# A two-layer encoder trunk in float32r parts: a quarter of the weights' low parts made by an accumulating DMA

## The chip, the cores and the metric

The kernel runs on one core of one Trainium2 chip. The core has five engines that work side by side: TensorE (PE, matrix products), VectorE (DVE), ScalarE (ACT), GpSimd (POOL) and SyncE (SP, which here only issues transfers). Sixteen DMA engines move data; they serve the queues of SP and of GpSimd alike. The metric is the time of one execution on the device in microseconds (us), the median over the runs. Lower is better.

## What is computed

Two layers of a post-norm encoder on one sequence of 256 tokens with 2048 features. Layer 0 mixes tokens by a stick-breaking attention, layer 1 by a multi-scale pooling.

```python
for i in range(DEPTH):                     # DEPTH = 2, ALPHA = (2 * DEPTH) ** 0.25
    x = layer_norm(ALPHA * x + 0.5 * swiglu(x, *ffn1[i]), *ln1[i])
    x = layer_norm(ALPHA * x + mixers[i](x), *ln2[i])
    x = layer_norm(ALPHA * x + 0.5 * swiglu(x, *ffn2[i]), *ln3[i])

def swiglu(x, w_in, w_out):                # w_in 2048 x 8192, w_out 4096 x 2048
    a, gate = jnp.split(x @ w_in, 2, axis=-1)
    return (jax.nn.silu(a) * gate) @ w_out
```

All is float32. Nearly all of the work is the product of x with about 495 MB of weights, each of which is read once.

## The kernel before, in words

**Parts.** TensorE multiplies in float32r, a float32 with a shortened mantissa. To keep float32's accuracy the kernel writes every operand as the sum of two float32r parts: `hi`, the value rounded, and `lo`, what the rounding left. A product is then hi\*hi + lo\*hi + hi\*lo. For the weights both parts are made on the chip, just ahead of their use.

**Chunks.** `chunk` (L117 of before) takes the next piece of a weight matrix: four tiles of 128 rows by 512 columns, 1 MB, loaded by one DMA on SP's queue into a buffer `raw` (three buffers). It is converted in two halves (j = 0, 1) of two tiles each: ScalarE copies the half to `whi` (a cast that rounds, L133), VectorE subtracts that from the raw half and writes `wlo` (L134). `whi` and `wlo` have five buffers each, so the conversion can run up to four halves ahead of the one in use. A `raw` buffer is free for the next load when both its halves have been converted, a `whi` or `wlo` buffer when TensorE has done its last product with it. There are 468 chunks, 936 halves.

**Products.** `gemm` makes 512 columns of a product, the columns with number `col`: it goes through the chunks r = 0 .. n-1 of the contraction (n = 4 for 2048 features, 8 for 4096) and sums in four PSUM banks, one for each 128 columns (f). In all chunks but the last the order is by tile, then by f, so that a half is used up before the next begins. In the last chunk the order is by f, then by tile, so that the four banks end one after the other and can be evacuated (`evac`); there both halves are in use until the chunk's end. The first products with x ahead of a layer norm sum all three parts in one bank (`one`). The values of the attention (`values`) and the last sublayer (`last`) have loops of their own around `chunk`.

**Around it.** ScalarE and VectorE also evacuate the banks, apply SiLU, the gates and the layer norms, and split x and the inner activations into parts. GpSimd does little: constants at the start, seven small powers for 1 / std (`rstd_of`), and eight transfers that spread the last layer norm's gain and bias over the partitions (`gb`). Each engine runs its instructions in a fixed order; that order is made at build time by a scheduler which plays the program through, from the program's order as the priority, and the waits on semaphores follow from who writes and reads which buffer.

Of the kernel before, what the change touches and what calls it, by code (L numbers as in the profile page):

```python
# [8 lines left out]
F32 = mybir.dt.float32  # L9
F32R = mybir.dt.float32r  # L10
AF = mybir.ActivationFunctionType
ALU = mybir.AluOpType
# [23 lines left out]
def trunk(ctx: ExitStack, tc: tile.TileContext, a: dict, out: bass.AP):  # L36
# [14 lines left out]

# [1 line left out]
    xq = [res.tile([P, 4, T], F32, tag=f"xq{q}", name=f"xq{q}") for q in range(4)]  # L53
    xf = [x[:, j] for x in xq for j in range(4)]
    # Its float32r parts, [hi | lo], each with room for the gain and bias of the layer norm.
    xsq = [res.tile([P, 4, 2, W], F32R, tag=f"xs{q}", name=f"xs{q}") for q in range(4)]
    xs = [x[:, j] for x in xsq for j in range(4)]
    whole = [x[:, :, :T] for x in xs]

# [1 line left out]
    mean_grp = const.tile([P, P], F32, name="mean_grp")  # L61
# [4 lines left out]
    nc.vector.memset(mcol, 1.0 / D)  # L66
    # The tensor engine runs at its full clock only after a while of work: products for
    # nothing, until the first data is here.
    idle = bank("idle")
# [5 lines left out]
    nc.gpsimd.memset(mhalf, -0.5)  # L75
    # tri[k', k] = 1 where k' >= k; past[k, q] = 1 where k < q, twice.
    tri = const.tile([P, P], F32, name="tri")
# [20 lines left out]
    def split(dst, hi_src, lo_src):  # L98
        """dst = [hi | lo] of float32r parts that add up to the source."""
        nc.scalar.copy(dst[:, 0], hi_src)  # L100
        nc.vector.tensor_tensor(out=dst[:, 1], in0=lo_src, in1=dst[:, 0].bitcast(F32), op=ALU.subtract)

    def split2(t, src):
        """xs of tiles t and t + 1, of two tiles side by side."""
        hi, lo = (xsq[t // 4][:, t % 4:t % 4 + 2, h, :T] for h in range(2))
        nc.scalar.copy(hi, src)
        nc.vector.tensor_tensor(out=lo, in0=src, in1=hi.bitcast(F32), op=ALU.subtract)

# [1 line left out]
    def load_x(q, j=None):  # L110
# [4 lines left out]

# [1 line left out]
    def chunk(w, r, c, fine=False, step=4):  # L117
        """Four 128-row tiles of 512 columns of w, in halves of hi and lo parts."""
        raw = raws.tile([P, 4, 512], F32, tag="raw", name="raw")
        if fine:  # L120
            for j in range(4):
                load_x(0, j)
                nc.sync.dma_start(raw[:, j], w[r, c, :, j])
        else:
            for j in range(0, 4, step):
                nc.sync.dma_start(raw[:, j:j + step], w[r, c, :, j:j + step])
        his, los = [], []
        for j in range(2):
            hi = whis.tile([P, 2, 512], F32R, tag="whi", name="whi")
            lo = wlos.tile([P, 2, 512], F32R, tag="wlo", name="wlo")  # L130
            for i in ((slice(0, 1), slice(1, 2)) if step < 4 else (slice(0, 2),)):
                src = raw[:, 2 * j:2 * j + 2][:, i]
                nc.scalar.copy(hi[:, i], src)  # L133
                nc.vector.tensor_tensor(out=lo[:, i], in0=src, in1=hi[:, i].bitcast(F32), op=ALU.subtract)  # L134
            his += [hi[:, i] for i in range(2)]
            los += [lo[:, i] for i in range(2)]
        return his, los

    def gemm(w, col, rhs, evac, hooks=None, load=False, one=0, r0=0):
        """Four 128-row tiles of (a 512-column block of w).T @ x, one bank each: hi*hi + lo*hi left,  # L140
        hi*lo right; or all in one sum of that many columns."""
        nk = len(rhs)
        n = nk // 4
        banks = None

        def mm(ps, hi, lo, f, kk):
            cs = slice(f * P, (f + 1) * P)
            first, last = kk == 0, kk == nk - 1
            x = rhs[kk]
            if one:  # L150
                nc.tensor.matmul(ps[:, :one], hi[:, cs], x[:, 0, :one], start=first, stop=False)  # L151
                nc.tensor.matmul(ps[:, :one], hi[:, cs], x[:, 1, :one], start=False, stop=False)  # L152
                nc.tensor.matmul(ps[:, :one], lo[:, cs], x[:, 0, :one], start=False, stop=last)  # L153
                return

            def high():
                nc.tensor.matmul(ps.rearrange("p (h n) -> p h n", h=2), hi[:, cs], x, start=first, stop=last)  # L157

            def low():
                nc.tensor.matmul(ps[:, :T], lo[:, cs], x[:, 0], start=False, stop=False)  # L160

            for go in ((high, low) if first else (low, high)):
                go()

        for c in range(n):
            if load and c > 0:
                load_x(c)
            his, los = chunk(w, r0 + c, col, fine=load and c == 0, step=2 if load else 4)
            if c == 0:
                banks = [bank(f"ps{f}") for f in range(4)]  # L170
            if c < n - 1:
                for k in range(4):
                    for f in range(4):
                        mm(banks[f], his[k], los[k], f, 4 * c + k)
            else:
                for f in range(4):
                    for k in range(4):
                        mm(banks[f], his[k], los[k], f, 4 * c + k)
                    evac(f, banks[f])
            if hooks and c in hooks:  # L180
                hooks[c]()

    def total(dst, ps, norm=None):
        """dst = left + right half of a product; or, of a raw one, what the layer norm makes of it,
        but for the bias that is returned."""
        if norm is not None:
# [9 lines left out]

# [1 line left out]
    EPS = LN_EPS / (ALPHA * ALPHA)  # L198
# [7 lines left out]
    class Norm:  # L206
        """LN of what x holds, less a shift: its statistics, 1 / std and -mean on all partitions,
        and its result, for four tiles at a time. Ahead of it, xs = [hi | lo] of gain * x."""

# [11 lines left out]
        def add(self, t):  # L221
            """Tiles t and t + 1."""
            q, j = divmod(t, 4)
# [14 lines left out]
        def stats(self):  # L238
            # Sums over the features, by token: means, then mean squares.
            s = self.sums  # L240
# [30 lines left out]
    def sublayer_end(w, rhs, factor, gname, bname, hooks=None, one=0):  # L271
        """x <- LN(ALPHA x + factor y): LN of x + (factor / ALPHA) y, with eps / ALPHA**2."""
        c = factor / ALPHA
# [3 lines left out]
        def shift_down():  # L277
            # The mean of the first group: from here on all is less that shift, which the
            # layer norm doesn't see, and the variance is free of cancellation.
            s0 = tmp.tile([P, T], F32, tag="half", name="s0")  # L280
# [23 lines left out]
    def ahead(norm, products, first=True, last=True):  # L304
        """Products (w, col, evac) with x ahead of its layer norm, which comes meanwhile:
        the statistics in the first of them, the result in the last."""
        for i, (w, col, evac) in enumerate(products):
# [6 lines left out]

# [1 line left out]
    def ffn_in(w_in, norm, hooks=None, npairs=1):  # L316
# [35 lines left out]

# [1 line left out]
    def attention(p, norm):  # L354
# [17 lines left out]
        def diag(x):  # L372
            """The two blocks where only some of the keys are past."""
            return x.rearrange("p (j q) -> p j q", j=3)[:, ::2]

        def scores(hg):
            def go():
                hs = range(4 * hg, 4 * hg + 4)
                with tc.manual_schedule(engines={mybir.EngineType.Activation}):
                    for h in hs:  # L380
                        # By key: keys 0..127 for all queries, keys 128..255 for the later queries.
                        ps = bank(f"z{h}")
# [6 lines left out]
                        nc.scalar.activation(sp[h], zs[h], AF.Abs)  # L389
                    # One table after the other.  # L390
                    for h in hs:
# [3 lines left out]
                for h in hs:  # L395
                    # softplus(z) of the past keys
                    nc.vector.scalar_tensor_tensor(out=sp[h], in0=zs[h], scalar=0.0, in1=sp[h], op0=ALU.max, op1=ALU.add)
# [4 lines left out]
        def weights(hg):  # L402
            def go():
# [7 lines left out]
                for h in hs:  # L411
                    # exp(min(log_w, 0))
                    lw[h] = scratch(28 + h % 4, F32, f"lw{h}")[:, :NZ]
# [38 lines left out]

# [1 line left out]
    def pooling(p, norm):  # L454
# [55 lines left out]

# [1 line left out]
    def last(p, norm):  # L512
# [115 lines left out]
```

## Time and profile before

| | |
|---|---|
| median of 2 runs | 2683.65 us (both runs the same) |
| span of the profiled execution | 2681.8 us; 1.85 us lie around it |
| TensorE products busy | 2666.7 us, 99% |
| TensorE weight loads busy (beside the products) | 2365.1 us, 88% |
| VectorE busy | 1675.7 us, 62% |
| ScalarE busy | 1365.4 us, 51% |
| GpSimd busy | 11.9 us |
| DMA | 499.61 MB, mean 186 GB/s |
| granted TensorE clock | 0.998 of full speed on average |

Busy times are sums over instructions; an engine can be busy without being what the end waits for. A wait names the engine whose work ended it. Times in the views are microseconds from the start of the span; PEld is TensorE's weight load, which runs beside the products.

### The profile page before, as it was taken

Reading aid. Unit: us, or ns where it says so; the run is one execution under the profiler, and the core shown is the slowest. Engines: PE = TensorE matmul, PEld = TensorE weight load, DVE = VectorE, ACT = ScalarE, POOL = GpSimd, SP = SyncE. Lnnn points to the kernel's source line nnn. Section 1 sums busy time; section 2 is a strip of 40 time slices with the busy share of each in tenths; the row PEclk is TensorE's granted clock in tenths of the full one; section 3 lists DMA queues with packets and bytes.
Section 4 is the critical chain, followed back from the end, with each engine's and each line's share of the span. In section 5 each row is a group of like instructions: output and inputs, shape, how many; then the busy total and the mean of one; then the engine's idle time right before and its main releaser. Section 6 shows DMA issues by size and latency. Waiting matters only on the chain.

```text
span 2681.8 us, 38727 instructions
## 1 busy us (share of the span) xinstructions
PE 2666.7 (99%) x15916; PEld 2365.1 (88%) x15916; DVE 1675.7 (62%) x2298; ACT 1365.4 (51%) x1990; POOL 11.9 (0%) x28
## 2 busy tenths in 40 slices
PE   9999999999999999999999999999999999999998
PEld 8888888899999888888988888889888998888886
DVE  6555556585686555565765555667878775555545
ACT  5444444467565444444654444445555565444432
POOL 0000000000000000000000000000000000000000
PEclk9999999999999999999999999999999999999999
DMA  7555555554455555555555555554555545555653
GB/s 255 188 188 187 189 188 189 189 174 162 153 190 183 187 186 186 199 177 201 173 189 189 189 189 189 189 189 170 192 189 176 201 174 182 186 186 187 228 193 126
DMA packets 71521, 499.61 MB, mean 186 GB/s; under 512 B 7984, under 2 KB 8624, under 8 KB 12080
## 3 DMA queue, kind: packets, MB, share of 16 engines
q1 hardware_dynamic: 70704, 495.05, 52.4%
q8 instruction: 124, 2.03, 0.3%
q0 software_dynamic: 640, 2.10, 0.2%
q14 instruction: 53, 0.43, 0.0%
HBM read 495.02 MB, written 2.10 MB: 185 GB/s over the span
## 4 chain that ended last, share of the span: by engine, by line
PE 99%; DVE 1%; DMA 0%; SPq 0%; ACT 0%; issue 0%; DVEq 0%; ACTq 0%
PE ps L157 50%; PE ps L160 26%; PE ps L152 5%; PE ps L151 5%; PE ps L153 5%; PE y L573 2%; PE y L572 2%; PE y L574 2%; PE v L430 1%; PE v L428 1%; PE v L429 1%; DMA xq<-in_x 0%; PE cum L407 0%; DVE z L547 0%; PE bc L257 0%; PE st L244 0%
## 5 line engine op out<-in xcount | busy, mean ns | idle before, releaser
L134 DVE TENSOR_TENSOR wlo<-raw,whi 128x1024 fp32r<-128x1024 f32 (+1 forms) x946 | 1144.3, 1212 | 905.8 <-ACT whi L133 901.2
L133 ACT CAST whi<-raw 128x1024 fp32r<-128x1024 f32 (+1 forms) x946 | 982.0, 1041 | 1080.1 <-PE ps L157 851.9
L157 PE MATMUL ps<-xs,whi 128*128 128x512 f32 x3968 | 1389.8, 396 | 1.1 <-ACT whi L133 0.7
L160 PE MATMUL ps<-xs,wlo 128*128 128x256 f32 x3968 | 1100.5, 280 | 1.0 <-DVE wlo L134 1.0
L157 PEld LDWEIGHTS ps<-xs,whi 128*128 128x128 f32 x3968 | 744.8, 189 | 173.4 <-ACT whi L133 1.0
L160 PEld LDWEIGHTS ps<-xs,wlo 128*128 128x128 f32 x3968 | 748.3, 189 | 7.3 <-DVE wlo L134 1.5
L157 PE MATMUL ps<-g,whi 128*128 128x512 f32 x1536 | 534.9, 394 | 0.0
L160 PE MATMUL ps<-g,wlo 128*128 128x256 f32 x1536 | 427.8, 280 | 0.0
L157 PEld LDWEIGHTS ps<-g,whi 128*128 128x128 f32 x1536 | 287.2, 187 | 65.3
L160 PEld LDWEIGHTS ps<-g,wlo 128*128 128x128 f32 x1536 | 289.7, 189 | 1.1
L152 PE MATMUL ps<-xs,whi 128*128 128x258 f32 (+1 forms) x896 | 252.7, 284 | 0.0
L151 PE MATMUL ps<-xs,whi 128*128 128x258 f32 (+1 forms) x896 | 251.7, 283 | 0.0
L153 PE MATMUL ps<-xs,wlo 128*128 128x258 f32 (+1 forms) x896 | 245.5, 282 | 0.0
L152 PEld LDWEIGHTS ps<-xs,whi 128*128 128x128 f32 x896 | 169.6, 189 | 0.2
L151 PEld LDWEIGHTS ps<-xs,whi 128*128 128x128 f32 x896 | 168.9, 188 | 0.0
L153 PEld LDWEIGHTS ps<-xs,wlo 128*128 128x128 f32 x896 | 167.6, 190 | 0.0
L194 ACT COPY half<-ps 128x256 f32<-128x256 f32 x264 | 97.1, 369 | 121.0 <-PE ps L157 119.6
L572 PE MATMUL y<-wlo,g 128*128 128x512 f32 x256 | 99.6, 389 | 0.0
L573 PE MATMUL y<-whi,g 128*128 128x512 f32 x256 | 99.6, 389 | 0.0
L574 PE MATMUL y<-whi,g 128*128 128x512 f32 x256 | 99.4, 389 | 0.0
L157 PE MATMUL ps<-y,whi 128*128 128x512 f32 x256 | 89.6, 396 | 0.0
L195 DVE TENSOR_TENSOR act<-ps,half 128x256 f32<-128x256 f32 x124 | 52.1, 421 | 46.6 <-ACT half L194 46.6
(151 smaller groups left out, 1677.0 us busy)
## 6 DMA issues: line engine op xcount, KB each, us to landing
raw<-in_l_ffn_w_in SPq DMA_DIRECT2D x252, 1024.0 KB, 4.8
raw<-in_l_ffn_w_out SPq DMA_DIRECT2D x127, 1024.0 KB, 4.8
raw<-in_l_pool_w_in SPq DMA_DIRECT2D x32, 1024.0 KB, 4.9
raw<-in_l_sb_w_qkv SPq DMA_DIRECT2D x24, 1024.0 KB, 4.8
raw<-in_l_pool_w_out SPq DMA_DIRECT2D x16, 1024.0 KB, 4.9
raw<-in_l_sb_w_o SPq DMA_DIRECT2D x8, 1024.0 KB, 4.9
raw<-in_l_pool_w_grp SPq DMA_DIRECT2D x4, 1024.0 KB, 4.9
raw<-in_l_ffn_w_in SPq DMA_DIRECT2D x6, 512.0 KB, 9.4
```

What stands on the lines that cost most here:

```text
L133: nc.scalar.copy(hi[:, i], src)
L134: nc.vector.tensor_tensor(out=lo[:, i], in0=src, in1=hi[:, i].bitcast(F32), op=ALU.subtract)
L151: nc.tensor.matmul(ps[:, :one], hi[:, cs], x[:, 0, :one], start=first, stop=False)
L152: nc.tensor.matmul(ps[:, :one], hi[:, cs], x[:, 1, :one], start=False, stop=False)
L153: nc.tensor.matmul(ps[:, :one], lo[:, cs], x[:, 0, :one], start=False, stop=last)
L157: nc.tensor.matmul(ps.rearrange("p (h n) -> p h n", h=2), hi[:, cs], x, start=first, stop=last)
L160: nc.tensor.matmul(ps[:, :T], lo[:, cs], x[:, 0], start=False, stop=False)
L194: nc.scalar.copy(t, ps[:, T:])
L195: nc.vector.tensor_tensor(out=dst, in0=ps[:, :T], in1=t, op=ALU.add)
L572: nc.tensor.matmul(ps[m], gh, lo, start=kk == 0, stop=False)
L573: nc.tensor.matmul(ps[m], gl, hi, start=False, stop=False)
L574: nc.tensor.matmul(ps[m], gh, hi, start=False, stop=kk == nk - 1)
```

## The change

In the second half of a chunk (j = 1), where r + c is odd (r the chunk's number in the contraction, c the column number) and the chunk is loaded in one piece (step = 4), `lo` is no longer made by VectorE. ScalarE writes the negative of the raw weights to `lo`; since `lo` is float32r, the write rounds, and what lies there is the negative high part. Then a DMA on GpSimd's queue adds the raw weights to it in place (`accum_op=ALU.add`), from the chip's own memory to the same memory: 128 partitions of 1024 elements, 512 KB. 232 of the 936 halves are made so, one in two chunks. The other changed lines only take out comments, so that line numbers behind it differ by five.

```diff
@@ chunk @@
                 src = raw[:, 2 * j:2 * j + 2][:, i]
                 nc.scalar.copy(hi[:, i], src)
-                nc.vector.tensor_tensor(out=lo[:, i], in0=src, in1=hi[:, i].bitcast(F32), op=ALU.subtract)
+                if j == 1 and (r + c) % 2 and step == 4:
+
+                    nc.scalar.activation(lo[:, i], src, AF.Copy, scale=-1.0)
+                    nc.gpsimd.dma_start(lo[:, i], src, accum_op=ALU.add)
+                else:
+                    nc.vector.tensor_tensor(out=lo[:, i], in0=src, in1=hi[:, i].bitcast(F32), op=ALU.subtract)
             his += [hi[:, i] for i in range(2)]
```

The first place is ScalarE in the first feed-forward sublayer, where the even column group 4 is prepared while the group ahead of it ends. `raw` 1765, 1811, 1853, 1895 of before are its four chunks; COPY `half` and CAST `g` belong to the evacuation of the group ahead. Before:

```order
L133 CAST whi_1813<-raw_1811 128x1024
L194 COPY half_1711<-ps0_1571 128x256
L194 COPY half_1727<-ps1_1572 128x256
L100 CAST g12_1709<-gate_1710 128x256
L194 COPY half_1743<-ps2_1573 128x256
L100 CAST g13_1725<-gate_1726 128x256
L133 CAST whi_1817<-raw_1811 128x1024
L194 COPY half_1759<-ps3_1574 128x256
L133 CAST whi_1855<-raw_1853 128x1024
```

And now the same place, where these chunks are `raw` 1779, 1825, 1868, 1910 and the ACTIVATE of L136 writes the negative:

```order
L133 CAST whi_1827<-raw_1825 128x1024
L199 COPY half_1725<-ps0_1584 128x256
L199 COPY half_1741<-ps1_1585 128x256
L100 CAST g12_1723<-gate_1724 128x256
L199 COPY half_1757<-ps2_1586 128x256
L100 CAST g13_1739<-gate_1740 128x256
L136 ACTIVATE wlo_1832<-raw_1825 128x1024
L133 CAST whi_1831<-raw_1825 128x1024
L199 COPY half_1773<-ps3_1587 128x256
L133 CAST whi_1870<-raw_1868 128x1024
```

The negative stands where the cast of that half stood, and the cast comes right behind it.

The second place is ScalarE at the start of the pooling layer, where the layer norm's result is applied (ACTIVATE `xq`, CAST `xs`) while the first products run. Before:

```order
L133 CAST whi_17388<-raw_17386 128x1024
L106 CAST xs0_80<-xq0_76 128x2x256
L218 CAST xs0_80<-vecs_119 128x4x2
L268 ACTIVATE xq2_78<-xq2_78,vecs_119 128x256 x2
L268 ACTIVATE xq3_79<-xq3_79,vecs_119 128x256 x4
L133 CAST whi_17392<-raw_17386 128x1024
L106 CAST xs1_81<-xq1_77 128x2x256
```

And now, with `raw` 17547 for the same chunk:

```order
L133 CAST whi_17549<-raw_17547 128x1024
L106 CAST xs0_80<-xq0_76 128x2x256
L223 CAST xs0_80<-vecs_119 128x4x2
L273 ACTIVATE xq2_78<-xq2_78,vecs_119 128x256 x2
L273 ACTIVATE xq3_79<-xq3_79,vecs_119 128x256 x4
L471 ACTIVATE u_17236<-u_17236,aux_17237 128x256
L133 CAST whi_17553<-raw_17547 128x1024
L106 CAST xs1_81<-xq1_77 128x2x256
L471 ACTIVATE u_17263<-u_17263,aux_17264 128x256
L136 ACTIVATE wlo_17554<-raw_17547 128x1024
```

Here the negative stands behind both casts of its chunk and behind other work; so it does in 41 of the 232 places.

The third place is GpSimd's whole order behind the constants; TENSOR_TENSOR is the power of `rstd_of`, DMA `gb` the gain and bias rows. Before:

```order
L85 AFFINE_SELECT past<-past 128x256
L201 TENSOR_TENSOR rn<-var,mhalf 128x2 x5
L534 DMA gb_23347<-in_l_ln_g 128x512 x4
L534 DMA gb_23352<-in_l_ln_b 128x512 x4
L201 TENSOR_TENSOR rs<-ve,mhalf 128x1 x2
```

And now:

```order
L85 AFFINE_SELECT past<-past 128x256
L137 DMA wlo<-raw 128x1024 x48
L206 TENSOR_TENSOR rn<-var,mhalf 128x2
L137 DMA wlo<-raw 128x1024 x16
L206 TENSOR_TENSOR rn<-var,mhalf 128x2
L137 DMA wlo<-raw 128x1024 x48
```

The transfers of the low parts stand between the powers, in the order of the chunks.

## Rows read from the trace of the kernel before

**Rows 1.** Page, part 1: busy us, share of the span, count, by engine
```profile
PE 2666.7 (99%) x15916; PEld 2365.1 (88%) x15916; DVE 1675.7 (62%) x2298; ACT 1365.4 (51%) x1990; POOL 11.9 (0%) x28
```

**Rows 2.** Page, part 4: the chain that ended last, by engine
```profile
PE 99%; DVE 1%; DMA 0%; SPq 0%; ACT 0%; issue 0%; DVEq 0%; ACTq 0%
```

**Rows 3.** Waits: who waited for whom; us in total, times, longest
```profile
DVE wlo L134 <- ACT whi L133: 901.2, 667, 5.1
ACT whi L133 <- PE ps L157: 851.9, 562, 4.2
...
PE ps L160 <- DVE wlo L134: 1.0, 1, 1.0
```

**Rows 4.** Groups by line and shape: count, busy us, mean ns, idle before
```profile
L134 DVE TENSOR_TENSOR wlo<-raw,whi 128x1024 fp32r<-128x1024 f32 x926 | 1131.2, 1223 | 898.9 <-ACT whi L133 894.6
...
L133 ACT CAST whi<-raw 128x1024 fp32r<-128x1024 f32 x926 | 970.4, 1050 | 1071.9 <-PE ps L157 851.9 <-PE y L574 93.8 <-PE ps L152 91.8
```

**Rows 5.** Page, parts 3 and 6: the load queue's share; one load, us to landing
```profile
q1 hardware_dynamic: 70704, 495.05, 52.4%
...
raw<-in_l_ffn_w_in SPq DMA_DIRECT2D x252, 1024.0 KB, 4.8
```

**Rows 6.** Timeline, ScalarE, even column group: start, us, instruction, idle before
```profile
188.46 1.05 ACT L133 CAST whi<-raw 128x1024 fp32r<-128x1024 f32 x1
...
197.57 1.05 ACT L133 CAST whi<-raw 128x1024 fp32r<-128x1024 f32 x1 [1.76 <-PE ps L157]
200.43 1.05 ACT L133 CAST whi<-raw 128x1024 fp32r<-128x1024 f32 x1 [1.81 <-PE ps L157]
```

**Rows 7.** Timeline, weight loads: first use of those two low parts
```profile
197.14 0.19 PEld L160 LDWEIGHTS ps<-xs,wlo 128*128 128x128 f32 x1
...
206.26 0.19 PEld L160 LDWEIGHTS ps<-xs,wlo 128*128 128x128 f32 x1
```

**Rows 8.** Timeline, ScalarE, odd column group: casts of the halves concerned
```profile
225.65 1.05 ACT L133 CAST whi<-raw 128x1024 fp32r<-128x1024 f32 x1 [1.72 <-PE ps L157]
...
236.89 1.05 ACT L133 CAST whi<-raw 128x1024 fp32r<-128x1024 f32 x1 [0.94 <-PE ps L157]
```

**Rows 9.** Timeline, weight loads: first use of those two low parts
```profile
236.46 0.19 PEld L160 LDWEIGHTS ps<-xs,wlo 128*128 128x128 f32 x1
...
247.68 0.19 PEld L160 LDWEIGHTS ps<-xs,wlo 128*128 128x128 f32 x1
```

**Rows 10.** Timeline, GpSimd: the first four issues of the gain rows
```profile
2479.26 2.35 POOL L534 DMA_DIRECT2D gb<-in_l_ln_g  x4 [334.72 <-PE ps L157]
```

**Rows 11.** DMA queues, 2479.3 to 2482.5: packets, MB, share of 16 engines
```profile
q1 hardware_dynamic: 133, 1.02, 86.2%
```

**Rows 12.** DMA queues, 2482.5 to 2488: the software queue
```profile
q0 software_dynamic: 320, 1.05, 63.9%
```

**Rows 13.** Tile gb: its transfers, from issue to landing
```profile
DMA to landing us min/median/max: 6.2/6.9/8.2
```

**Rows 14.** DMA queues, 180 to 212: the load queue
```profile
q1 hardware_dynamic: 818, 5.92, 51.6%
```

**Rows 15.** Timeline, ScalarE: casts of three halves with short windows
```profile
30.78 2.00 ACT L133 CAST whi<-raw 128x1024 fp32r<-128x1024 f32 x2
...
1918.66 1.06 ACT L133 CAST whi<-raw 128x1024 fp32r<-128x1024 f32 x1 [0.58 <-PE ps L157]
...
2650.93 1.05 ACT L133 CAST whi<-raw 128x1024 fp32r<-128x1024 f32 x1 [1.67 <-PE y L574]
```

**Rows 16.** Timeline, weight loads: first use of those three low parts
```profile
39.92 0.19 PEld L160 LDWEIGHTS ps<-xs,wlo 128*128 128x128 f32 x1
...
1924.21 0.19 PEld L160 LDWEIGHTS ps<-xs,wlo 128*128 128x128 f32 x1
...
2658.67 0.19 PEld L572 LDWEIGHTS y<-wlo,g 128*128 128x128 f32 x1
```

## Prediction

> **What bounds the kernel now.** I read the busy shares first. TensorE works 99% of the span, VectorE and ScalarE about half of it [rows 1]. The chain that ended last says the same in another way: 99% of it is TensorE [rows 2]. So an instruction saved elsewhere is worth nothing unless TensorE waits for it. The waits give the direction: VectorE waits 901 us in all for ScalarE's high parts, ScalarE 852 us for TensorE to give back a buffer, while TensorE waits 1.0 us, once, for a low part [rows 3]. The preparation of weights runs as far ahead as its five buffers allow and then stands still. TensorE's whole idle time is 2681.8 - 2666.7 = 15 us, and no change can win more than that, 0.6%.
>
> What matters for this change is therefore a single number: how long a low part may take before TensorE wants it. I call it the window: from the end of the moment at which the negative can be written to the weight load that first reads that low part. The negative needs the raw weights and a free buffer, just as the cast of the high part does, so it can start when the cast of that half started before. In a gemm with an even column number the transferred halves are those of its second and fourth chunk. The cast of the first of these began at 188.46 and took 1.05 [rows 6], the weight load came at 197.14 [rows 7]: window 7.6 us. For the other one, 197.57 + 1.05 to 206.26: 7.6 again. In a gemm with an odd column number it is the first and third chunk: 225.65 + 1.05 to 236.46 and 236.89 + 1.05 to 247.68 [rows 8, 9], both 9.7 us. The even windows are shorter because the last chunk of a product is used four columns at a time, so that both its halves come free only at its end, and because a fourth chunk's second half is wanted early for the same reason. By the loops, 116 transfers are of even columns and 116 of odd ones.
>
> Some windows are shorter still, where ScalarE is late with the cast: I compared the start of the cast with the first weight load for all 232 halves, and 13 lie below 7.3 us. The first in time is the second cast of the pair that begins at 30.78 (it ends at 32.78, used at 39.92: 7.1), the shortest begins at 1918.66 (used at 1924.21: 4.5), the last at 2650.93 (used at 2658.67: 6.7) [rows 15, 16].
>
> **The change part by part.** VectorE loses 232 subtractions of 1223 ns [rows 4], 284 us; it was idle for more than that, so this is worth 0. ScalarE gets 232 more instructions. The negative has the cast's shape, which takes 1050 ns, so 244 us, 51% to 60% of the span. It stood waiting for TensorE 852 us, which covers this: 0. In the regular groups the order shows the negative ahead of its own half's cast, so the cast comes 1.05 us later, with a window of its own that is over a microsecond longer than the one I worked out for the low part. Where the order has the negative behind both casts and other work (41 of 232 places, mostly at the layer norms), its window shrinks by another 1.05.
>
> GpSimd issues 232 transfers. Four issues of the gain rows took 2.35 us [rows 10], 0.6 each, 140 us in all on an engine that was empty: 0. Its seven small power steps now stand behind such issues; at worst each is held for one half's time, 2.9 us (197.57 to 200.43 [rows 6]), some 20 us; I take 0, since one issue takes 0.6.
>
> The DMA engines carry 0.524 MB (512 KB) more per transfer. In a quiet stretch the hardware queue moved 5.92 MB in 51.6% of 32 us, 359 GB/s [rows 14]: a plain copy would keep all sixteen busy for 1.46 us. An accumulating one isn't in this trace. From below it costs that copy. From above: with n copies' worth per transfer the engines' share becomes 52.4% [rows 5] + n x 232 x 1.46 / 2682 = 52.4% + 12.6% n, full at n = 3.8. I take n = 2, because two streams have to be read (raw and the negative) for one that is written: 2.9 us, share 78%.
>
> The Trainium skill (Collectives: The Full Stack, The bandwidth ceiling: the fold count and why AG ≠ RS ≠ AR) says that an add inside the DMA is free but needs two source reads, and gives 32.35 against 62.28 GB/s for the two. By that estimate n would be 1.9 and a landing 0.1 us shorter than with my 2; no run here shows it.
>
> A transfer from GpSimd's queue also starts late. The first gain row was issued at 2479.26 [rows 10], and up to 2482.5 only the hardware queue has packets [rows 11]; after that the software queue has 1.05 MB [rows 12]. That is 3.2 us from issue to first packet. So landing after the negative: 3.2 + 2.9 + 0.3 for the hand-over and the report of the end (my estimate) = 6.4 us; bounds 3.2 + 1.5 + 0.3 = 5.0 below, 3.2 + 5.5 (n = 3.8) + 0.3 = 9.0 above. The nearest measured thing, a 256 KB row transfer on that queue with loads beside it, landed in 6.2 to 8.2 us [rows 13].
>
> The Trainium skill (DMA: Bandwidth & Descriptors, Anatomy of one DMA) fits such a transfer with 2.0 us plus its bytes at 436 GB/s, 3.2 us for 512 KB. The trace disagrees: 3.2 us pass here before a first packet moves, so the row is used. By the page's estimate hardly a window would be missed.
>
> Collisions: loads are issued in order, and a raw buffer is now free only when its transfer has landed. In an even group the first transfer lands at 189.5 + 6.4 = 195.9; two loads of 2.9 us each then go at once. A load lands in 4.8 us [rows 5], so about 1.9 pass before its packets: they flow from 197.8 to 203.6. The second transfer's packets start at 198.6 + 3.3 = 201.9 and share 1.7 us: 0.9 later, landing at 205.9, needed at 206.26. It fits, narrowly. In odd groups 2 us and more remain. A late load has slack too: landing at 200.7 it meets the cast that started at 200.43 before [rows 6], and that half too is wanted more than eight microseconds later.
>
> The sum: subtraction 0, negative 0, issues 0, regular windows 0. The 13 short windows have their middle at 5.8, about 5.1 with the negative behind the cast: 13 x (6.4 - 5.1) = 17 us. The profiled execution (span 2681.8, 1.85 around it) is the median run itself: 2683.65 + 17 = 2700.
>
> **What a miss costs.** Within a pair the second transfer starts before the first one's stall, so its need moves with the stall and the pair pays once. Every microsecond of landing past 7.6 costs 58 pairs x 1 us = 58 us, past 9.7 twice that. 2% is 54 us, about what a measurement of this kernel can tell from no change; it is reached at a landing of about 8.2 us.
>
> **The rivals.**
> Slower: the transfer takes a quarter of a copy's rate (n = 4). Then it needs 5.8 us, lands 9.3 after the negative, 1.7 late in the even columns: 58 x 1.7 = 99, and 13 x 4.2 = 55 at the short windows, 2840 us. The queues would stand at 103%, which alone means 2760. For it speaks that the margin of my forecast is 1.2 us in one place and 0.4 in another; against it, that nothing in an addition asks for four passes. It decides from a landing of 8.2 us on. Chance 0.23.
> Much slower: landing at 12 us (many small descriptors, or a longer start than that of a plain transfer): 58 x 4.4 + 58 x 2.3 + 13 x 7 = 480, about 3160 us. Nothing in the trace excludes it, as no accumulating transfer is in it. Chance 0.18.
> Faster: VectorE's relief reaches TensorE. At most 15 us of idle time exist, so 2668 at best; over 2% can't come from there. Chance 0.02.
>
> **How the numbers follow.** Forecast (landing 5 to about 8 us; 2680 to 2735) 0.57, slower 0.23, much slower 0.18, faster 0.02. I give 2700. The range reaches from 2680 over the first slower case, to 2860, and leaves out the much slower one. Faster by over 2%: 0.02; within 2%: 0.57; slower: 0.41.
>
> **What the new profile would show.** Right: low-part transfers landing in 6 to 7 us from issue, DMA share between 65 and 80%, TensorE's waits for the transfer under 30 us and at the layer norms and the pooling layer, VectorE near 1390 us busy, ScalarE near 1610. Wrong: waits of TensorE for the low part in every even group (rate or start mis-sized, visible as landing over 7.6), a DMA share near 100% (n of 4 or more), or waits for power steps behind GpSimd's issues.

## The result, and the profile after

| | before | after |
|---|---|---|
| median | 2683.65 us | 2729.25 us (2 runs, 2725.56 and 2732.94) |
| ratio | | 1.017, 95% interval 1.0153 to 1.0187 |
| profiled execution, its span | 2681.8 us | 2723.9 us (time 2725.56) |

The change costs 46 us, 1.7%. That lies under the 2% bound and inside the forecast's own range (2680 to 2735), but it is nearly three times the 16 us of the sum. The page of the changed kernel: part 1 (busy us by engine), part 3 (queues: packets, MB, share of 16 engines), part 4 (the chain that ended last), groups of part 5, and part 6 (issues, KB, us to landing).

```profile
PE 2677.0 (98%) x15916; PEld 2367.0 (87%) x15916; DVE 1407.1 (52%) x2066; ACT 1571.4 (58%) x2222; POOL 212.9 (8%) x260
...
q1 hardware_dynamic: 70704, 495.05, 51.2%
q0 software_dynamic: 34048, 123.75, 23.3%
...
PE 85%; DMA 9%; issue 3%; ACT 2%; DVE 1%; SPq 0%; DVEq 0%; POOLq 0%; ACTq 0%; POOL 0%
...
L137 POOL DMA_DIRECT2D wlo<-raw x232 | 201.1, 867 | 2465.7 <-ACT wlo L136 1620.5
...
L136 ACT ACTIVATE wlo<-raw 128x1024 fp32r<-128x1024 f32 x232 | 245.5, 1058 | 152.0 <-PE ps L165 135.2
...
raw<-in_l_ffn_w_in SPq DMA_DIRECT2D x252, 1024.0 KB, 5.6
...
wlo<-raw POOLq DMA_DIRECT2D x232, 512.0 KB, 5.8
```

The engines are as forecast: VectorE 1407 us (about 1390 was said), ScalarE 1571 (1610), the DMA share 51.2 + 23.3 = 74.5% (78%). What is new is in the chain: 99% TensorE before [rows 2], now 85%, with 9% of DMA. The waits of the changed kernel (who for whom: us in total, times, longest) and the landing times of the tile `wlo` tell which DMA:

```profile
ACT whi L133 <- PE ps L162: 382.8, 275, 6.3
ACT whi L133 <- DMA raw<-in_l_ffn_w_in: 140.2, 54, 4.9
...
PE ps L165 <- DMA wlo<-raw: 20.5, 16, 3.6
...
POOL rn L206 <- DVE var L256: 9.0, 4, 2.3
...
PE ps L158 <- DMA wlo<-raw: 6.2, 4, 2.6
...
PE y L577 <- DMA wlo<-raw: 3.9, 2, 2.5
```

```profile
DMA to landing us min/median/max: 4.5/5.8/11.4
```

TensorE waits 20.5 + 6.2 + 3.9 = 30.6 us for transfers, 22 times, where it waited 1.0 us for a low part before [rows 3]. A landing takes from 4.5 to 11.4 us after its issue. ScalarE, which stood before a full buffer for 852 us [rows 3], now does so for 383, and also waits for loads; TensorE itself waits 1.0 us, once, for a high part.

The last product ends 41.8 us later than before (2711.7 against 2669.9). 30.6 us of that are these waits. Some 5 us are lost where the granted clock fell behind three of them; I have not traced the other 6 singly. The stretches around the first fall, all engines (length; busy us and count of PE, PEld, DVE, ACT and POOL; granted clock, DMA share, GB/s), and products there:

```profile
601.00:603.00 2.00, 2.00 (x18) 1.83 (x16) 2.00 (x6) 1.10 (x5) 0.00 (x0) 1.00 1.02 287
605.70:609.10 3.40, 3.40 (x16) 3.40 (x17) 0.72 (x3) 0.74 (x2) 0.86 (x1) 0.50 1.04 373
609.20:611.20 2.00, 2.00 (x19) 2.00 (x18) 0.94 (x1) 2.00 (x4) 0.00 (x0) 1.00 1.00 225
```

```profile
605.60 1.20 PE L158 MATMUL ps<-xs,wlo 128*128 128x256 f32 x4 [2.56 <-DMA wlo<-raw]
606.59 0.41 PE L156 MATMUL ps<-xs,whi 128*128 128x256 f32 x1
...
609.36 0.28 PE L158 MATMUL ps<-xs,wlo 128*128 128x256 f32 x1
```

TensorE had stood 2.56 us for a transfer; then 0.50 was granted (1.2 of 2.4 GHz) from 605.7 to 609.1, products began every 0.21 us in place of 0.12, and 16 x 0.09, about 1.5 us, were lost on top of the wait. The same happened after the waits of 3.63 us (at 1908.9) and 2.97 us (2086.9). The kernel before has no such fall between its start and its end.

### The profile page after: what moved, and what is told of

Same layout as the page of the kernel before. It is cut to its first block, busy times and chain, and to the rows that moved or that the text cites. A ratio compares the mean times of both kernels' runs of the same rounds, so it can differ in the third digit from the quotient of the medians.

```text
span 2723.9 us, 39725 instructions
## 1 busy us (share of the span) xinstructions
PE 2677.0 (98%) x15916; PEld 2367.0 (87%) x15916; DVE 1407.1 (52%) x2066; ACT 1571.4 (58%) x2222; POOL 212.9 (8%) x260
## 3 DMA queue, kind: packets, MB, share of 16 engines
q1 hardware_dynamic: 70704, 495.05, 51.2%
q0 software_dynamic: 34048, 123.75, 23.3%
## 4 chain that ended last, share of the span: by engine, by line
PE 85%; DMA 9%; issue 3%; ACT 2%; DVE 1%; SPq 0%; DVEq 0%; POOLq 0%; ACTq 0%; POOL 0%
PE ps L162 45%; PE ps L165 23%; DMA wlo<-raw 7%; PE ps L158 3%; PE ps L157 3%; PE ps L156 3%; PE y L577 2%; PE y L578 2%; PE y L579 2%; DMA raw<-in_l_ffn_w_in 1%; DMA raw<-in_l_ffn_w_out 1%; ACT whi L133 1%; ACT wlo L136 1%; PE v L435 1%; PE v L433 1%
## 5 line engine op out<-in xcount | busy, mean ns | idle before, releaser
L139 DVE TENSOR_TENSOR wlo<-raw,whi 128x1024 fp32r<-128x1024 f32 (+1 forms) x714 | 859.6, 1208 | 1094.0 <-ACT whi L133 1088.1
L165 PE MATMUL ps<-xs,wlo 128*128 128x256 f32 x3968 | 1102.1, 281 | 13.4 <-DMA wlo<-raw 11.5
L137 POOL DMA_DIRECT2D wlo<-raw x232 | 201.1, 867 | 2465.7 <-ACT wlo L136 1620.5
L136 ACT ACTIVATE wlo<-raw 128x1024 fp32r<-128x1024 f32 x232 | 245.5, 1058 | 152.0 <-PE ps L165 135.2
```

The costliest lines, as they stand in the source:

```text
L136: nc.scalar.activation(lo[:, i], src, AF.Copy, scale=-1.0)
L137: nc.gpsimd.dma_start(lo[:, i], src, accum_op=ALU.add)
```

## Where the long landings come from

A regular even column group, that of [rows 6, 7]: timelines of ScalarE, GpSimd and the weight loads (start, us, instruction, idle before), then the software queue from 191 to 196, with one transfer in it.

```profile
189.33 1.06 ACT L136 ACTIVATE wlo<-raw 128x1024 fp32r<-128x1024 f32 x1
...
198.29 1.06 ACT L136 ACTIVATE wlo<-raw 128x1024 fp32r<-128x1024 f32 x1 [1.52 <-PE ps L165]
```

```profile
190.69 0.87 POOL L137 DMA_DIRECT2D wlo<-raw  x1 [18.24 <-ACT wlo L136]
199.65 0.87 POOL L137 DMA_DIRECT2D wlo<-raw  x1 [8.09 <-ACT wlo L136]
```

```profile
198.09 0.19 PEld L165 LDWEIGHTS ps<-xs,wlo 128*128 128x128 f32 x1
...
207.22 0.19 PEld L165 LDWEIGHTS ps<-xs,wlo 128*128 128x128 f32 x1
```

```profile
q0 software_dynamic: 144, 0.52, 55.0%
```

The negatives end at 190.39 and 199.35, so the windows are 7.7 and 7.9 us: the forecast's 7.6. The first transfer, alone, lands 4.5 us after its issue. Its packets fill the engines for 55% of 5 us, 2.75 us; start and report take the other 1.75. The second shares the engines with a load and lands 6.2 after its issue, 6.5 after the negative (7.3 was forecast), 1.4 before its use. Both fit, and by such groups the change would cost nothing.

An odd column group fits as well, as long as it begins well: at 227.72 to 261.42 four transfers land within 5.0 to 5.5 us, and windows are 10.0. But another one of the same form, from 983.54 on, looks so (GpSimd's issues, then SP's load issues):

```profile
983.54 0.86 POOL L137 DMA_DIRECT2D wlo<-raw  x1 [4.75 <-ACT wlo L136]
994.78 0.86 POOL L137 DMA_DIRECT2D wlo<-raw  x1 [10.38 <-DVE gate L339]
1006.12 0.86 POOL L137 DMA_DIRECT2D wlo<-raw  x1 [10.48 <-ACT wlo L136]
1018.19 0.86 POOL L137 DMA_DIRECT2D wlo<-raw  x1 [11.21 <-ACT wlo L136]
```

```profile
993.58 0.80 SPq L126 DMA_DIRECT2D raw<-in_l_ffn_w_in  x2
...
1004.75 0.80 SPq L126 DMA_DIRECT2D raw<-in_l_ffn_w_in  x2
...
1016.27 0.81 SPq L126 DMA_DIRECT2D raw<-in_l_ffn_w_in  x2
```

The first transfer starts beside a load (issued at 983.34) and lands 9.9 us after its issue, at 993.4. Until then it holds a raw buffer, and SP's queue, which runs in order, holds the next load too. At 993.58 both loads, 2 MB, go out, 1.2 us ahead of the next transfer, which now shares the engines with them through its whole way and lands after 9.8 us, at 1004.6; at 1004.75 the next pair of loads goes out. The delay reproduces itself from chunk to chunk. Of the 48 landings of over 8.9 us, 40 had a pair of loads issued 0.2 to 3.5 us ahead of the transfer. 35 of the 48 lie in odd columns, most of them in the window of 10 us, where they are just in time: TensorE waits 0.4 us in all for odd columns with such a window. The last chunk of an even column has about 8 us, and there they are not in time. One such place is the last chunk of column 2 in the first feed-forward sublayer's second product. Its transfer goes out 1.5 and 1.1 us behind a pair of loads, lands after 10.05 us and finds a window of 8.3 (GpSimd, TensorE):

```profile
491.51 0.87 POOL L137 DMA_DIRECT2D wlo<-raw  x1 [10.07 <-ACT wlo L136]
```

```profile
501.61 0.38 PE L165 MATMUL ps<-g,wlo 128*128 128x256 f32 x1 [2.07 <-DMA wlo<-raw]
```

TensorE waits 13.1 us in all in ten such chunks, 14.6 in seven places with windows under 7.3 us, and 3.0 in the rest. The longest landing of all is near the end of the kernel (SP, GpSimd, TensorE; then the queues from 2565 to 2577):

```profile
2564.59 0.80 SPq L126 DMA_DIRECT2D raw<-in_l_ffn_w_out  x2
```

```profile
2565.35 0.86 POOL L137 DMA_DIRECT2D wlo<-raw  x1 [9.22 <-ACT wlo L136]
```

```profile
2576.77 0.50 PE L577 MATMUL y<-wlo,g 128*128 128x512 f32 x1 [2.46 <-DMA wlo<-raw]
```

```profile
q1 hardware_dynamic: 288, 2.10, 53.2%
q0 software_dynamic: 262, 1.00, 41.7%
```

Loads and transfers (the next one is issued at 2572.53) have the engines busy for 95% of these 12 us between them, and the transfer of 2565.35 takes 11.4 us where a lone one takes 4.5. The Trainium skill (Trainium Kernel Development and Optimization, Key Constraints) says that transfers of all issuing queues run on the same sixteen engines and interleave; these rows agree.

My theory: the loss is the lengthening of landings by loads beside them, a small part short windows, and on top the falls of the clock behind long waits. Rivals: ScalarE's extra work or the changed order; the transfer by itself; a fixed cost of every transfer. The trace gives the theory its size: with a landing 4.8 us after the negative in every window of the changed kernel, about 6 of the 30.6 us of waits would be left.

## The experiments

Edits are against the changed kernel. Every kernel was timed against the kernel before, on the same chip (before: 2683.5 to 2683.9 us).

**The negative alone.** The transfer is left out, so `lo` stays the negative high part, and the raw weights are never added to it.

```diff
-                    nc.gpsimd.dma_start(lo[:, i], src, accum_op=ALU.add)
```

> The transfer is left out; ScalarE still writes the negative, so that a quarter of the low parts are the negative high parts and the product is not the reference's. It shows what ScalarE's 232 extra instructions and the new order cost by themselves. Theories A and B: within 4 us of the kernel before, 2680 to 2688, and no granted clock under full speed between start and end. Theory C (ScalarE's extra work or its order makes TensorE wait): 2695 or more.

Measured: 2683.23 us, ratio 0.9999 (0.9990 to 1.0009), no wait of TensorE over 1.2 us. So ScalarE's 245 us, the order, and VectorE's relief together are worth nothing, in either direction. All of the loss hangs on the transfers.

**A copy in place of the addition.** `lo` is then the raw weights: same bytes written, same starts.

```diff
-                    nc.gpsimd.dma_start(lo[:, i], src, accum_op=ALU.add)
+                    nc.gpsimd.dma_start(lo[:, i], src)
```

> The transfer copies the raw weights over the negative instead of adding to it, so a quarter of the low parts are wrong; ScalarE's work, issues and waits stay. It measures the price of the addition. If the add costs a second read: packets of the software queue go from 328 ns to about 160, its share of the DMA engines from 23% to about 12%, landing alone from 4.5 to about 3.2 us, and TensorE's waits to under half (below 12 us), 2690 to 2700. If the start of a transfer from GpSimd's queue is what costs: landing stays at 4 us or more and the time within 10 us of the changed kernel, 2715 or more.

Measured: 2692.95 us, ratio 1.0037 (1.0022 to 1.0052). The queue's row of that kernel, and its landings:

```profile
q0 software_dynamic: 34048, 123.75, 12.7%
```

```profile
DMA to landing us min/median/max: 2.9/3.7/8.1
```

```profile
PE ps L165 <- DMA wlo<-raw: 5.4, 2, 4.6
...
PE ps L158 <- DMA wlo<-raw: 1.2, 1, 1.2
```

Without the gain rows (0.2%) the copy keeps all engines busy for 12.5% x 2690.8 / 232 = 1.45 us, just the 1.46 worked out from [rows 14]; the addition for 23.1% x 2723.9 / 232 = 2.71, 1.87 times as long. That is about what a second read would add, though no view shows the reads as such. Waits for transfers fall to 6.6 us, and four fifths of the loss go. The clock falls once, at the wait of 4.6 us.

**The first half in place of the second.** My first idea of the collisions was that the second half's transfer, which holds the raw buffer to the end, brings the pairs of loads about. With the first half the chunk's own second cast comes later, and windows should be 10 us nearly everywhere.

```diff
-                if j == 1 and (r + c) % 2 and step == 4:
+                if j == 0 and (r + c) % 2 and step == 4:
```

> The transfer makes the low part of the first half of the same chunks (j = 0) instead of the second. Each low part is still made in full; nothing else is moved. A raw buffer is then held mainly by VectorE's second half, as before the change, so loads are no longer held back by a transfer and should not go out in pairs. Theory A (TensorE's new waits come mostly from transfers that meet two weight loads on the DMA engines): nearly all landings between 4.5 and 6 us from issue (changed kernel: median 5.8, up to 11.4), TensorE waits for transfers under 8 us in all, time 2685 to 2695. Theory B (the transfer by itself is too long for its windows): landings spread as in the changed kernel, 2700 to 2720. Theory C (ScalarE writes the negative too late at the layer norms): landings near 4.5 to 6, but some 13 us of waits stay at the layer norms and the pooling layer, 2695 to 2705.

Measured: 2717.96 us, ratio 1.0126 (1.0105 to 1.0146). Windows did grow (median 9.97; in even columns 10.0 in place of 7.9), but landings grew with them and TensorE waits 23.6 us for transfers. Its landings:

```profile
DMA to landing us min/median/max: 4.5/6.8/11.3
```

Theory A missed: the time is in theory B's range, the landings spread as B said, and this run alone could not tell the two apart; the one without loads, below, decides. The idea that the hold to the end of the chunk is the one cause of the collisions falls: 200 of the 232 landings now take over 6 us, against 105 in the changed kernel.

**Own low buffers.** Transferred halves get two low buffers of their own, the others the remaining three, so that the negative can be written a chunk earlier.

```diff
-    wlos = ctx.enter_context(tc.tile_pool(name="wlos", bufs=5))
+    wlos = ctx.enter_context(tc.tile_pool(name="wlos", bufs=3))
+    sums_ = ctx.enter_context(tc.tile_pool(name="sums_", bufs=2))
...
-            lo = wlos.tile([P, 2, 512], F32R, tag="wlo", name="wlo")
+            moved = j == 1 and (r + c) % 2 and step == 4
+            lo = (sums_ if moved else wlos).tile([P, 2, 512], F32R, tag="wlo", name="wlo")
```

> The low parts that a transfer makes get two buffers of their own, and three are left for the others (five in all, as in the changed kernel). The negative then needn't wait for the buffer of five halves ago and can be written as soon as the raw weights are there; the loads are held back by the landing as in the changed kernel. Theory A (collisions with loads): landings still spread up to 9 us and more, but the windows are 2 to 5 us longer, so TensorE's waits fall under 10 us, 2685 to 2697. Theory B (transfer by itself too long): the same fall. Theory C (ScalarE late): waits of some 13 us stay at the layer norms, 2697 to 2710.

Measured: 2691.24 us, ratio 1.0033 (1.0020 to 1.0046). Landings are as long as before (4.5/6.1/11.5), but the windows, from the end of the negative to the weight load, have their middle at 13.3 us in place of 9.7. No product waits for a transfer, and a weight load does so once:

```profile
PEld ps L167 <- DMA wlo<-raw: 0.3, 1, 0.3
```

No clock fall is left. The last product ends at 2670.7, against 2669.9 before. What remains is behind it: 17.5 us to the end in place of 11.9. I put that down to the last chunks' lack of low buffers; the next run tries it.

**Own low buffers, shared out anew at the end.** As above (the diff is against that version, whose own pool is called `moved_lo` here), but a late chunk of the last sublayer takes the buffer of its second half from those of the transferred halves.

```diff
-            lo = (sums_ if moved else wlos).tile([P, 2, 512], F32R, tag="wlo", name="wlo")
+            lo = (moved_lo if moved or (spare and j == 1) else wlos).tile([P, 2, 512], F32R, tag="wlo", name="wlo")
...
+                parts = chunk(w_out, cc, q, step=2 if q == 3 and cc == n - 1 else 4, spare=q == 3 and cc == n - 3)
```

> The transferred halves have two low-part buffers of their own, the rest the other three, and in the last four chunks of the last sublayer the halves share them in such a way that five stand ready at the end, as in the kernel before. With its own buffers alone the transfers cost 8 us, 5.6 of it behind the last product (17.5 us in place of 11.9). Theory: wider windows (middle 12 us in place of 8.5) outlast the longest landing of 11.4 us, TensorE waits for no transfer, the tail is 11.9 us again, time 2684 to 2687, ratio to the kernel before 1.000 to 1.001. Rival: the tail comes from the transfers beside the last loads and not from the buffers, then it stays near 17 us and the time at 2690.

Measured: 2690.0 us (2686.95 to 2696.74, 9 runs), ratio 1.0025 (1.0015 to 1.0034). The profiled execution is the fastest one, 2686.95: TensorE waits 0.5 us for transfers and ends 1.3 us later than before, and the tail is 14.1 us, between the two expectations. The median is the rival's 2690, not the theory's 2684 to 2687. What the other executions, up to 10 us slower, lose stays open, and with it how much of the tail came from the buffers. It doesn't beat the kernel before, and by the 15 us of idle time it couldn't by much.

**Without loads.** After the first gemm the same weight tiles stay in SBUF and are read again: all casts, negatives, transfers and products remain.

```diff
-    raws = ctx.enter_context(tc.tile_pool(name="raws", bufs=3))
+    raws = ctx.enter_context(tc.tile_pool(name="raws", bufs=1))
...
+        plain = not fine and step == 4
+        if plain and len(kept) == 2:
+            raw = kept[turn[0] % 2]
+            turn[0] += 1
+        else:
+            raw = (keep if plain else raws).tile([P, 4, 512], F32, tag=f"k{len(kept)}" if plain else "raw", name="raw")
...
+        if plain:
+            pass
...
```

> The changed kernel without its weight loads: every gemm after the first reads two weight tiles that stay in SBUF, so the products are of wrong weights and the output is not the reference's; the casts, negatives, transfers, subtractions and all products are made as before. It tells whether the long landings of the changed kernel come from the loads that run beside the transfers. Theory (collision): all landings at 4.5 to 4.7 us from issue, none over 6; TensorE's waits for a transfer fall from 30.6 us to at most 8 (with a landing of 4.5 in every window of the changed kernel's trace, 6.3 us would be left), the granted clock stays whole, time 2684 to 2695. Rival (the transfers are slow by themselves, or held up by GpSimd's or ScalarE's work): landings spread up to 10 us as before, waits stay near 30 us, time 2715 to 2730.

Measured: 2702.07 us, ratio 1.0068 (1.0052 to 1.0083): slower than the theory said, faster than the rival. The landings have their middle at 4.5 us, three quarters of them under 4.6 and 11 of 232 over 6 (up to 6.7), where the theory had none; the waits for transfers, 6.2 us in four places, are the theory's. The clock did not stay whole: it fell behind the waits of 1.73 us (at 1357.2) and 2.34 us (at 1902.7). But this version had a single raw buffer for its start, and 10.9 of its 20.7 us at the last product were lost before 40 us, with TensorE standing 8.7 us at 22.5 for VectorE. So once more with three:

```diff
...
+        if plain and len(kept) == 3:
+            raw = kept[turn[0] % 3]
+            turn[0] += 1
+        else:
+            raw = raws.tile([P, 4, 512], F32, tag="raw", name="raw")
...
```

> The kernel without weight loads again, with three raw buffers at the start as the changed kernel has (the first version had one, and its trace shows 10.9 us lost before 40 us, while the first products' weights came in one at a time). After the first gemm the three tiles stay and are read in turn; the products are of wrong weights, all instructions but the loads are there. Collision theory: what is left of the loss is the short windows alone, 6 to 9 us: landings 4.5 us, TensorE's waits for transfers 5 to 8 us, one or two falls of the granted clock at 1.7 us each, no loss before 40 us; time 2689 to 2694. Rival (the 10.9 us belong to the transfers and not to the missing buffers): 2699 to 2704 again.

Measured: 2691.19 us (2690.46 to 2693.59, 7 runs), ratio 1.0030 (1.0018 to 1.0041). Landings and waits of that kernel:

```profile
DMA to landing us min/median/max: 4.5/4.5/6.4
```

```profile
PE ps L176 <- DMA wlo<-raw: 5.9, 4, 2.3
...
PE ps L169 <- DMA wlo<-raw: 1.0, 2, 0.8
```

6.9 us of waits, 7.3 us of loss, no fall of the clock (its longest waits for transfers are 1.75 and 2.28 us), and nothing over 0.5 us lost before 40 us, so the rival falls. The windows are those of the changed kernel (middle 9.8 and 9.7 us), so it is the landings that differ: without loads beside them the same transfers cost 7 us, with them 46.

**Half the bytes.** One of the two tiles of a half goes by the transfer, VectorE adds the other to the negative.

```diff
-                    nc.gpsimd.dma_start(lo[:, i], src, accum_op=ALU.add)
+                    nc.gpsimd.dma_start(lo[:, :1], src[:, :1], accum_op=ALU.add)
+                    nc.vector.tensor_tensor(out=lo[:, 1:], in0=src[:, 1:], in1=lo[:, 1:].bitcast(F32), op=ALU.add)
```

> Only the first of the two tiles of a transferred half (256 KB) goes by the accumulating transfer, the other is added by VectorE to the negative that ScalarE wrote. Half the bytes in the same 232 places, with the same starts. Collision theory: a landing alone 3.1 us (4.5 less half of the 2.7 us in which packets flow), beside loads 4 to 7; TensorE's waits for a transfer less than half of 30.6 us, no fall of the granted clock, time 2690 to 2702. Rival (a start or a fixed cost of each transfer sets the stalls): landings shorter by under 1 us, waits over 20 us, time over 2712.

Measured: 2691.68 us, ratio 1.0030 (1.0019 to 1.0041).

```profile
DMA to landing us min/median/max: 3.2/3.8/7.7
```

```profile
PE ps L166 <- DMA wlo<-raw: 3.0, 3, 2.2
...
PE ps L159 <- DMA wlo<-raw: 2.3, 2, 2.0
```

The waits for transfers are 5.3 us, under a fifth of 30.6, though as many transfers start at the same places. A fixed cost of each is not what stalls TensorE. Past the first 12 us the clock fell once all the same, behind the wait of 2.2 us (at 1348.0), where no fall was expected.

**Twice as many.** The second half of every chunk is transferred, 463 in all.

```diff
-                if j == 1 and (r + c) % 2 and step == 4:
+                if j == 1 and step == 4:
```

> The second half of every chunk goes by the transfer, not of every other one: twice as many, about 464, half of all low parts. DMA share by the changed kernel's rows: 51% of loads and two times 23% of transfers, 98%. Collision theory: loads and transfers always lie beside each other, landings mostly 8 to 11 us, beyond the windows of 7.6 and 9.7 us in many groups; TensorE waits in most gemms, the DMA engines become the bound or nearly so, time 2800 to 2950. Rival (a stall belongs to a transfer and not to what lies beside it): the loss just doubles, 46 us to about 92, 2775 us, landings with the same middle of 5.8 us.

Measured: 2958.55 us (2946.41 to 2970.81), ratio 1.1025 (1.0994 to 1.1056). The chain of that kernel, and the largest group of TensorE's waits:

```profile
DMA 47%; PE 33%; issue 13%; ACT 4%; DVE 2%; POOL 0%; SPq 0%; POOLq 0%; ACTq 0%; DVEq 0%
```

```profile
PE ps L165 <- DMA wlo<-raw: 132.4, 101, 5.7
```

Twice the transfers cost six times as much, 275 us, a little more than the theory's range. The middle landing is 6.9 us, not the 8 to 11 that I expected, and the DMA share 92.5%; the clock falls 29 times. Loss by transfer is no constant: it grows with what lies beside it on the engines.

## Why the prediction was off

**What held.** TensorE is the bound, and nothing saved elsewhere is worth anything: the negative alone shows 0 for the subtraction and for ScalarE. So is GpSimd's issue, though it took 0.87 us, not 0.6 from [rows 10]. The power steps do not wait behind issues: they wait for VectorE, as before. The windows were right to 0.3 us, 7.7 to 10.0. The transfer's weight was right: n = 2 was taken, 1.87 measured. The estimate of 1.9 from the Trainium skill (Collectives: The Full Stack, The bandwidth ceiling: the fold count and why AG ≠ RS ≠ AR) agrees with what the copy and the addition show here.

**The start was mis-sized, to the good side.** The 3.2 us before the first packet came from the gain rows [rows 10 to 12]. The transfers of this change needed 1.75 us for start and report together, so that a lone landing is 0.3 + 4.5 = 4.8 us after the negative, not 6.4. (The 0.3 for the hand-over stood there without a row; measured from the end of the negative to the issue it is 0.3.) The prediction set aside the estimate of the Trainium skill (DMA: Bandwidth & Descriptors, Anatomy of one DMA) of 3.2 us for a plain 512 KB; the copy's 2.9 us is near that estimate. Why the gain rows start later wasn't tried.

**The short windows** were charged 17 us. The kernel without loads shows what they cost at a lone landing, 7 us: 13 such windows were counted, only six of them stalled, as the landing was shorter.

**The step that failed is the one on collisions, which put the regular windows at 0 in the sum.** It had the mechanism (a raw buffer held until the landing, two loads going out at once) and worked it through in one even group, where it found 0.9 us (6.2 - 4.5 = 1.7 measured) and the second transfer in time ("it fits, narrowly"). It took that one group for all, and said that in odd groups 2 us and more remain. In the changed kernel nothing remains in many odd groups: the loads are held until just before the next transfer, the collision lasts for the whole transfer, and the long landing sets up the next, 9 to 10 us in a window of 10. They cost TensorE only 0.4 us themselves, but the same chain runs on into even columns and through the longer products, and at their last chunk the narrow fit breaks: landings of 8.1 to 11.4 us in nine of the ten places where TensorE waits there, with 6.4 in the sum. Windows of 7.3 us and more, charged 0, cost 16.1 of the 30.6 us of waits, 13.1 of it in last chunks of even columns; the short ones cost 14.6, of which about 6 would be left at a lone landing. The price is the difference between 46 and 7 us, 38 us. In the profiled execution it stands as 30.6 - 6.9 = 24 us of waits, 3 x 1.5 = 5 us at the lowered clock, and some 5 us not traced singly. That the repetition is due to the hold alone is read from times in the trace; no run isolated it, and the run with the first half shows that collisions come also where the transfer is not the chunk's last.

**What was missing altogether** is that a long wait can cost more than itself by the clock; those 5 us are part of the 38. The two errors to either side (10 us too much for the short windows, 38 too little for collisions) bring 2700 to about 2729. That this still lies inside 2680 to 2735 is in part luck, since the one hides some of the other. None of the rivals came: the rate was not a quarter, and the landing not 12 us in the middle, but its upper tail reached 11.4, and a tail is enough where TensorE is 99% busy. One sum was off, too: by its own terms the forecast reaches 54 us at a landing of 7.9 us, not 8.2 (13 x (7.9 - 5.1) + 58 x (7.9 - 7.6)).

## What to carry to other kernels

Where a DMA is put between two engines' work, compare the window with the landing beside the largest transfers that can run at that moment, not with the mean share of the queues; 75% of the engines were in use here and landings still more than doubled. Ask what buffer the transfer holds, whose load waits for it, and whether that load then starts just ahead of the next transfer: such a delay can feed itself, as at 983 us here. A cure is a longer window (buffers of its own for what is transferred) or smaller transfers, and each took the loss here from 46 to 8 us; neither gave a gain, since the engine that was relieved was not the bound.

## What the runs showed of the hardware

- An accumulating transfer of 512 KB within SBUF took 4.5 us alone, a copying one 2.9 us, an accumulating one of 256 KB 3.2 us. GpSimd issued the accumulating ones in 0.86 to 0.87 us, the copy in 0.53.
- Beside weight loads the accumulating one took up to 11.4 us in the changed kernel, and a load issued 0.3 us ahead of it 11.3.
- Behind some single waits of TensorE the granted clock fell to 0.5 (1.2 of 2.4 GHz): in the changed kernel behind 2.56, 2.97 and 3.63 us, in the first kernel without loads behind 1.73 us. Behind others it did not: 3.18 us (at 2215.1) and 2.46 us (at 2576.8) in the changed kernel, 1.75 and 2.28 us in the second kernel without loads. The kernel before, the one with the negative alone and the first with own low buffers, whose longest wait is 1.12 us, had no fall between start and end.
- The executions of one kernel with transfers lie 2 to 24 us apart, those of the kernel before under 2.
